# Two of w_out's operands split into halves beside the convolutions, the attention norm's weight folded into w_out, and the steps of the output projection's first pair moved

## The chip, the cores and the metric

The kernel runs on one core of a Trainium2 chip. The metric is the device time of one execution in microseconds. Five engines work side by side, each in the order of its own queue: TensorE (PE, with its weight loads as PEld), VectorE (DVE), ScalarE (ACT), GpSimd (POOL) and SyncE (SP), which here issues the transfers (DMA). Results of TensorE lie in PSUM banks until another engine reads them.

## The reference

One encoder layer on 2048 tokens of width 1024, in float32. The change touches the part from the two norms to the output projection:

```python
att = banded_attention(q_a, k_a, v_a, sink)            # 8 heads of 64
att = rms_norm(att, g_attn_out)                        # (2048, 512)
h_m = rms_norm(h_fwd + h_bwd, g_mlstm_out)             # 4 heads of 128
h_m = sigmoid(o_m) * h_m                               # (2048, 512)
mix = concatenate([att, h_m], axis=-1) @ w_out         # (1024, 1024)
x = x + gate1 * mix
...
```

Ahead of it stand the modulation, the first norm, one input projection, a convolution of width 3 along the tokens for the mLSTM's q and k, the mLSTM in both directions and the banded attention; behind it a SwiGLU layer and the last norm.

## The kernel before

**Arithmetic.** A float32 product is made of three TensorE matmuls of halves (`mm3`, L56 to L58): hi by hi, lo by hi, hi by lo. An operand is split into halves by a ScalarE copy that rounds (hi) and a VectorE subtraction (lo = value − hi).

**Stages**, in the order of TensorE: modulation, first norm and the projections in natural layout (to about 180 us); the convolutions of q and k (about 181 to 243); the mLSTM, head by head (to about 570); the attention (to about 790); the output projection (about 815 to 990); the SwiGLU layer (to the end). Gaps of one stage are filled with matmuls of the next, by a queue `fill` of which `pull(n)` takes n steps. From the convolutions on, VectorE, ScalarE, POOL and SP execute in the order in which the code is written (`manual_schedule`); so where a step stands among the pulls sets its place in each queue.

**The convolutions** run in blocks of 512 tokens: 24 matmuls (L498) into one of two PSUM banks (tag "g"), then ScalarE takes the middle tap out of the bank (L525), ScalarE mends the edges (L526 to L529), and VectorE adds the two outer taps (L512, L513), after which the bank is free for the block after next. A loop of 252 pulls drives this window, and at pull i it also advances two lists of side steps that name their own due pulls by `yield`: `gates()` and `w_out_ops()`.

**w_out's operands.** The output projection is computed with 7 products in place of 8 on 2x2 blocks (a Strassen scheme), for each pair of 128-token blocks: 8 pairs. Its 7 weight operands (u = 0 to 6) are blocks of gate1·w_out and differences of them. `w_out_ops()` makes them in 8 chunks n of 128 rows by 2x256 columns: two loads `bx`, `by`, of w_out's rows of the attention half and of the mLSTM half, a multiplication of each by the gate on POOL (L944, L946), four subtractions on POOL (L957) into `ta` and `tb`, and stores to `wo_d` in DRAM. Chunk n's steps are due from pull 16 + 26n (+10 from n = 4). The two last differences, u = 4 and u = 6, lie in `tb`. The stores of the four differences wait in `out_` until the next chunk (L949), just ahead of the loads for the chunk after that (L922).

**The output projection** (`out_proj`). For product u, `start_wo(u)` loads the operand from `wo_d` as values, and `finish_wo(u)` splits it (L1046 on ScalarE, L1047 on VectorE); u = 5 and u = 6 are split inside the first pair (L1516, L1519). A product is 12 matmuls; b1, b2 and b5 are the three banks in which the seven accumulate, and after each product VectorE adds the bank onto the residual rows `xr` (L1224):

```python
for u, (ps, first, i, m) in enumerate(((b1, True, 0, M0), (b2, True, 0, M0), (b1, False, 0, M1), (b5, True, 1, M1),
                                       (b1, False, 1, M1), (b5, False, 0, M1), (b1, False, 1, M0))):
```

The token operands belong to a `Pair`: `load_a`, `load_m` and `load_gate` load the attention, mLSTM and output gate rows of 256 tokens, `square` and `columns` make the attention's sums of squares (ScalarE L1075, POOL L1076/L1077, TensorE L1125), `scale` multiplies the attention rows by 1/rms and the norm's weight (L1092), `gate` applies the output gate (L1095), `sums`, `s1`, `s4` form block sums on POOL, and `hi`/`lo` split one of the seven operands (L1114 on ScalarE, L1118 on VectorE). While pair p is multiplied, the loop of 28 pulls (i = 0 to 27) prepares pair p+1 (`nxt`) and the sums of squares of p+2 (`nx2`); for p = 0 some of pair 0's own operands are still split in it (`cur.both()`).

Of the kernel before, what the change touches and what calls it, by code (L numbers as in the profile page):

```python
# [36 lines left out]
def hybrid_layer_kernel(  # L37
# [35 lines left out]
    wo_d = dp.tile([7, 4, P, 512], F32, name="wo_d")  # L73
    a_d = dp.tile([7, DFF // P // 2, P, 2, 512], F32, name="a_d")
# [857 lines left out]
    def w_out_ops():  # L932
# [5 lines left out]
        out_ = ()  # L938
        for n, (c_, k) in enumerate(at_):
            at = 16 + 26 * n + 10 * (n > 3)  # L940
            cs = slice(c_ * 256, (c_ + 1) * 256)
            yield at + 3
            bx, by = ready.popleft()
            pool.tensor_tensor(bx, bx, gb[c_], MUL)  # L944
            yield at + 6
            pool.tensor_tensor(by, by, gb[c_], MUL)  # L946
            yield at + 8
            for o in out_:
                sp.dma_start(*o)  # L949
            yield at + 11  # L950
# [3 lines left out]
            tb = s2.tile([P, 2, 256], F32, tag="hst", name="ts")  # L954
            for t, f, g in ((ta[:, 1], bx[:, 1], bx[:, 0]), (tb[:, 0], by[:, 1], bx[:, 1]),
                            (ta[:, 0], by[:, 1], ta[:, 1]), (tb[:, 1], by[:, 0], ta[:, 0])):
                pool.tensor_tensor(t, f, g, SUB)  # L957
# [3 lines left out]
            out_ = [(wo_d[2:4, k, :, cs].rearrange("u p c -> p u c"), ta), (wo_d[4, k][:, cs], tb[:, 0]), (wo_d[6, k][:, cs], tb[:, 1])]  # L961
# [74 lines left out]
    wo = []  # L1036

    def start_wo(u):
        hl = [[big(4 * u + 2 * z + i, "wo") for i in range(2)] for z in range(2)]
        wo.append(hl)  # L1040
        for i in range(2):
            sp.dma_start(hl[1][i].bitcast(F32), wo_d[u, 2 * i:2 * i + 2].rearrange("k p t -> p k t"))
# [8 lines left out]
    class Pair:  # L1051
# [33 lines left out]
        def scale(self):  # L1085
# [5 lines left out]
            for k in range(4):  # L1091
                dve.scalar_tensor_tensor(self.a[:, :, k], self.a[:, :, k], cols[:, O_GA + k:O_GA + k + 1], rb, MUL, MUL)  # L1092
# [143 lines left out]
    nx2.load_m()  # L1236
    nx2.load_gate()
    xr = [load_xr(nxt.tt)]
# [8 lines left out]
    for u in (2, 3):  # L1247
        start_wo(u)
    pull(10)
# [10 lines left out]
    nx2.diagonal(rsqrt(mx, ps[:, :2], 2, 512, "ar"), diag())  # L1260
    finish_wo(2)
    finish_fill(lasts[2])
    for u in (4, 5):
        start_wo(u)
    xr.append(load_xr(nxt.tt + 1))
    nx3.load_a()
    finish_wo(3)
# [3 lines left out]
    finish_wo(4)  # L1271
# [206 lines left out]
    HI, LO = (5, 12, 17, 19, 21, 23, 25), (5, 13, 18, 20, 22, 24, 26)  # L1478
    FIRST = (1, 2, 5, 8, 16, 20, 24)
    rows = None  # L1480
    for p in range(NPR):
# [15 lines left out]
        for i in range(28):  # L1497
# [15 lines left out]
            if p == 0:  # L1513
                if i in (6, 14):
# [449 lines left out]
```

## Time and profile before

| what | value |
|---|---|
| median of 3 runs | 2263.45 us (2263.4, 2265.4, 2263.45) |
| profiled execution | 2268.64 us, span 2266.8 us, mean granted TensorE clock 0.995 |
| TensorE busy | 2223.8 us, 98% |
| VectorE, ScalarE, POOL busy | 1611.1, 1060.3, 1040.6 us (71%, 47%, 46%) |
| DMA | 391.28 MB, 173 GB/s on average |

The span runs from the first to the last record of the profiled execution; some 1.8 us of its time lie around it. In the trace a row is: start, duration (of the whole group where xN stands), engine, line, operation, out<-in, shape, and in brackets the idle time of that engine just before, with what ended it. A window's row has, for each engine, the busy time in the window and the number of instructions, and at its end the granted clock, DMA's busy share and GB/s.

### The profile page before, as it was taken

What the parts mean: (1) busy time and instruction counts of PE and PEld (TensorE: products, weight loads), DVE (VectorE), ACT (ScalarE), POOL (GpSimd) and SP (SyncE); (2) the same over time, 40 slices, a digit from 0 to 9 for tenths busy, and PEclk for the clock granted to TensorE, in tenths of its full rate; (3) what the DMA queues carried; (4) which work ended last, traced back from release to release, by engine and by line L of the source; (5) the groups of instructions that cost most, each with busy time, mean ns of one, the idle gap of its engine ahead of it and who ended that gap; (6) DMA issues with size and microseconds to landing.
All of it is one profiled execution on the core that took longest, in us unless ns stands there. A gap on an engine that the chain in (4) does not pass through costs nothing.

```text
span 2266.8 us, 32424 instructions
## 1 busy us (share of the span) xinstructions
PE 2223.8 (98%) x10822; PEld 1858.7 (82%) x10822; DVE 1611.1 (71%) x2944; ACT 1060.3 (47%) x2206; POOL 1040.6 (46%) x914
## 2 busy tenths in 40 slices
PE   6999999999999999999999999999999999999998
PEld 4997888888888878888888888888888888878887
DVE  6787577656688877886767786766666665785694
ACT  5433565654677746354444444433333333233452
POOL 1006635334344333436666674457566654692020
PEclk9999999999999999999999999999999999999999
DMA  8476755586666576764343454433333374542462
GB/s 329 161 244 209 246 166 168 182 240 180 205 186 183 174 243 207 268 235 150 108 149 112 158 181 164 157 98 111 98 112 98 112 260 142 176 142 94 144 217 93
DMA packets 352811, 391.28 MB, mean 173 GB/s; under 512 B 21260, under 2 KB 251004, under 8 KB 352644
## 3 DMA queue, kind: packets, MB, share of 16 engines
q1 hardware_dynamic: 352420, 389.18, 52.6%
q8 instruction: 85, 1.39, 0.2%
q14 instruction: 82, 0.67, 0.1%
q10 hardware_dynamic: 224, 0.04, 0.0%
HBM read 269.95 MB, written 119.19 MB: 172 GB/s over the span
## 4 chain that ended last, share of the span: by engine, by line
PE 88%; DVE 4%; ACT 3%; DMA 2%; issue 1%; POOL 1%; SPq 0%; ACTq 0%; POOLq 0%; DVEq 0%
PE gps L498 14%; PE fp L56 12%; PE fp L57 12%; PE fp L58 12%; PE fo L56 6%; PE fo L58 6%; PE fo L57 6%; PE ops L56 2%; PE ops L58 2%; PE ops L57 2%; PE kvp L622 1%; PE num L709 1%; PE num L711 1%; PE atp L805 1%; ACT ap L788 1%
## 5 line engine op out<-in xcount | busy, mean ns | idle before, releaser
L498 PE MATMUL gps<-hT,whi 128*128 128x512 f32 x1088 | 396.5, 419 | 0.3 <-DVE cacc L513 0.3
L56 PE MATMUL fo<-w,ah 128*128 128x512 f32 x616 | 239.9, 389 | 1.0 <-DVE rb L1876 1.0
L58 PE MATMUL fo<-w,al 128*128 128x512 f32 x616 | 239.9, 389 | 0.1
L57 PE MATMUL fo<-w,ah 128*128 128x512 f32 x616 | 239.7, 389 | 0.0
L498 PE MATMUL gps<-hT,wlo 128*128 128x512 f32 x544 | 226.7, 417 | 0.0
L498 PEld LDWEIGHTS gps<-hT,whi 128*128 128x128 f32 x1088 | 200.2, 190 | 24.7 <-DVE cacc L513 0.7
L56 PE MATMUL fp<-T,S 128*128 128x512 f32 x528 | 206.7, 391 | 0.3 <-ACT s L1610 0.3
L57 PE MATMUL fp<-T,S 128*128 128x512 f32 x528 | 205.6, 389 | 0.0
L58 PE MATMUL fp<-T,S 128*128 128x512 f32 x528 | 205.4, 389 | 0.0
L1718 DVE TENSOR_TENSOR al<-al,ah 128x1024 fp32r<-128x1024 f32 x77 | 117.4, 1530 | 108.0 <-ACT ah L1717 108.0
L1717 ACT ACTIVATE ah<-al 128x1024 fp32r<-128x1024 f32 x77 | 81.6, 1060 | 182.8 <-DMA al<-a_d 180.3
L1453 DVE TENSOR_TENSOR S<-sf,S 128x512 fp32r<-128x512 f32 x86 | 129.8, 1547 | 34.4 <-ACT S L1452 34.2
L1453 DVE TENSOR_TENSOR A<-graw,A 128x512 fp32r<-128x512 f32 x86 | 130.8, 1541 | 13.2 <-ACT A L1452 12.8
L58 PE MATMUL fp<-B,A 128*128 128x512 f32 x352 | 136.9, 389 | 0.0
L56 PE MATMUL fp<-B,A 128*128 128x512 f32 x352 | 136.9, 389 | 0.0
L57 PE MATMUL fp<-B,A 128*128 128x512 f32 x352 | 136.9, 389 | 0.0
L56 PEld LDWEIGHTS fo<-w,ah 128*128 128x128 f32 x616 | 115.6, 188 | 25.4 <-DVE rb L1876 1.8
L58 PEld LDWEIGHTS fo<-w,al 128*128 128x128 f32 x616 | 115.6, 188 | 24.7 <-DVE al L1718 0.5
L57 PEld LDWEIGHTS fo<-w,ah 128*128 128x128 f32 x616 | 115.6, 188 | 24.2
L1620 DVE SCALAR_TENSOR_TENSOR g<-t,g 128x512 f32<-128x512 f32 x44 | 41.8, 950 | 131.3 <-ACT t L1619 131.3
L798 POOL TENSOR_SCALAR ap<-ap,adn 128x384 f32<-128x384 f32 (+1 forms) x128 | 73.5, 594 | 125.7 <-PE atp L805 58.6
L1457 POOL TENSOR_TENSOR sf<-A,A22r 128x512 f32<-128x512 f32 x42 | 58.1, 1383 | 145.5 <-DMA A22r<-in_w_ffn_in_dram 118.5
(427 smaller groups left out, 6142.2 us busy)
## 6 DMA issues: line engine op xcount, KB each, us to landing
al<-a_d SPq DMA_DIRECT2D x77, 512.0 KB, 3.8
wmod<-in_w_mod_dram SPq DMA_DIRECT2D x48, 512.0 KB, 7.6
graw<-in_w_ffn_in_dram SPq DMA_DIRECT2D x43, 512.0 KB, 3.9
a_d<-ka SPq DMA_DIRECT2D x66, 256.0 KB, 4.7
bc<-bc_d SPq DMA_DIRECT2D x64, 256.0 KB, 3.7
hop_d<-n SPq DMA_DIRECT2D x56, 256.0 KB, 4.0
a_d<-u SPq DMA_DIRECT2D x55, 256.0 KB, 4.6
mqk<-qk_d SPq DMA_DIRECT2D x44, 256.0 KB, 3.8
```

Of the source, the lines that this page charges most:

```text
L56: pe.matmul(o, lh, rh, start=first, stop=False, skip_group_check=skip)
L57: pe.matmul(o, lh, rl, start=False, stop=False, skip_group_check=skip)
L58: pe.matmul(o, ll, rh, start=False, stop=last, skip_group_check=skip)
L498: pe.matmul(ps, w[i == 2][:, k, :], hT[n](i == 1, k), start=(k == 0 and i == 0), stop=(k == KT - 1 and i == 2))
L622: pe.matmul(kvp[:, :129], kn, vw, start=True, stop=True)
L709: pe.matmul(num[:, d, :129], sc[:, d, :], va_c, start=True, stop=st is None)
L798: pool.tensor_scalar(self.p[g][:, :self.NK], self.p[g][:, :self.NK], dn[:, g:g + 1], 0.0, MUL, ADD)
L1453: dve.tensor_tensor(t[:, 1, :], f, t[:, 0, :].bitcast(F32), SUB)
L1457: add.tensor_tensor(f1, a21, a22, ADD)
L1620: dve.scalar_tensor_tensor(g0, t0, 1.0, g0, ADD, MUL)
L1717: act.activation(ah, al.bitcast(F32), AF.Copy)
L1718: dve.tensor_tensor(al, al.bitcast(F32), ah.bitcast(F32), SUB)
```

## The change

1. In `w_out_ops()`, `tb` is split in place: `last_split` copies its two parts to `woh` on ScalarE and subtracts on VectorE, at pull at+5 of the next chunk; the stores of u = 4 and u = 6 go as halves, to `wo_d` (hi) and to a new DRAM tensor `wol_d` (lo). They are four stores where two were.
2. `bx` is multiplied by the attention norm's weight on ScalarE (at+9), between POOL's multiplication and POOL's subtractions. `Pair.scale` loses that factor: four VectorE operations become one, with the 1/rms row broadcast over the four 128-blocks.
3. `start_wo` loads both halves for u = 4 and u = 6; no split of them is left in or ahead of the first pair.
4. Loads ahead of the output projection are issued in another order (u = 2 and 3 before xr and the mLSTM rows; 5 before 4), and the splits of u = 2 and 3 stand one place later.
5. In the first pair, `cur.both()` moves from steps 3, 12, 13 to 0, 2, 13; wo5's subtraction is halved between steps 8 and 11; the squares for pair 2 move from step 15 to 9 (into a buffer of pool `w1`, which therefore lives on to step 22); `gate` and `sums` move by one step, and the `hi`/`lo` steps by one to three.

```diff
     wo_d = dp.tile([7, 4, P, 512], F32, name="wo_d")
+    wol_d = dp.tile([2, 4, P, 512], F32, name="wol_d")
...
         out_ = ()
+
+        cs = None
+
+        def last_split(k, cs, tb):
+            r = []
+            for z, tag in enumerate(("sc", "qs")):
+                hi, lo = s2.tile([P, 256], F32R, tag=tag, name="woh"), tb[:, z]
+                act.activation(hi, lo.bitcast(F32), AF.Copy)
+                dve.tensor_tensor(lo, lo.bitcast(F32), hi.bitcast(F32), SUB)
+                r += [(wo_d[4 + 2 * z, k][:, cs], hi.bitcast(F32)), (wol_d[z, k][:, cs], lo.bitcast(F32))]
+            return r
+
         for n, (c_, k) in enumerate(at_):
             at = 16 + 26 * n + 10 * (n > 3)
...
+            cs_, cs = cs, slice(c_ * 256, (c_ + 1) * 256)
             bx, by = ready.popleft()
             pool.tensor_tensor(bx, bx, gb[c_], MUL)
+            if n:
+                yield at + 5
+                out_ += last_split(at_[n - 1][1], cs_, tb)
             yield at + 6
             pool.tensor_tensor(by, by, gb[c_], MUL)
             yield at + 8
             for o in out_:
                 sp.dma_start(*o)
+            yield at + 9
+            act.activation(bx, bx, AF.Copy, scale=cols[:, O_GA + k:O_GA + k + 1])
             yield at + 11
             if 0 < n < len(at_) - 1:
                 ready.append(w_out_load(*at_[n + 1]))
             ta = s2.tile([P, 2, 256], F32, tag="bc", name="ts", bufs=3)
-            tb = s2.tile([P, 2, 256], F32, tag="hst", name="ts")
-            for t, f, g in ((ta[:, 1], bx[:, 1], bx[:, 0]), (tb[:, 0], by[:, 1], bx[:, 1]),
-                            (ta[:, 0], by[:, 1], ta[:, 1]), (tb[:, 1], by[:, 0], ta[:, 0])):
+            tb = s2.tile([P, 2, 256], F32R, tag="hst", name="ts")
+            tf = tb.bitcast(F32)
+            for t, f, g in ((ta[:, 1], bx[:, 1], bx[:, 0]), (tf[:, 0], by[:, 1], bx[:, 1]),
+                            (ta[:, 0], by[:, 1], ta[:, 1]), (tf[:, 1], by[:, 0], ta[:, 0])):
                 pool.tensor_tensor(t, f, g, SUB)
             yield at + 19
             for u, t in ((0, bx[:, 0]), (1, by[:, 0]), (5, by[:, 1])):
                 sp.dma_start(wo_d[u, k][:, cs], t)
-            out_ = [(wo_d[2:4, k, :, cs].rearrange("u p c -> p u c"), ta), (wo_d[4, k][:, cs], tb[:, 0]), (wo_d[6, k][:, cs], tb[:, 1])]
+            out_ = [(wo_d[2:4, k, :, cs].rearrange("u p c -> p u c"), ta)]
+        yield at + 27
+        out_ += last_split(k, cs, tb)
         yield at + 34
         for o in out_:
             sp.dma_start(*o)
...
+    wo = {}
 
     def start_wo(u):
         hl = [[big(4 * u + 2 * z + i, "wo") for i in range(2)] for z in range(2)]
-        wo.append(hl)
+        wo[u] = hl
         for i in range(2):
-            sp.dma_start(hl[1][i].bitcast(F32), wo_d[u, 2 * i:2 * i + 2].rearrange("k p t -> p k t"))
+            for t, d in ((hl[0], wo_d[u]), (hl[1], wol_d[u // 2 - 2])) if u in (4, 6) else ((hl[1], wo_d[u]),):
+                sp.dma_start(t[i].bitcast(F32), d[2 * i:2 * i + 2].rearrange("k p t -> p k t"))
 
     def finish_wo(u):
         for hi, lo in zip(*wo[u]):
...
-            for k in range(4):
-                dve.scalar_tensor_tensor(self.a[:, :, k], self.a[:, :, k], cols[:, O_GA + k:O_GA + k + 1], rb, MUL, MUL)
+            dve.tensor_tensor(self.a, self.a, rb.unsqueeze(2).to_broadcast([P, 2, 4, P]), MUL)
 
...
     nx2.load_a()
-    nx2.load_m()
-    nx2.load_gate()
-    xr = [load_xr(nxt.tt)]
     ps = bank("a", "aps")
     for i in range(2):
         pe.matmul(ps[:, i:i + 1], nxt.t[:, 2 + i], ones[:, 0:1], start=True, stop=True)
...
         nx2.square(i, sq[:, i])
     for u in (2, 3):
         start_wo(u)
+    xr = [load_xr(nxt.tt)]
+    nx2.load_m()
     pull(10)
     nxt.scale()
     nxt.sums(nxt.t.rearrange("p k t -> p (k t)"))
...
     nx2.diagonal(rsqrt(mx, ps[:, :2], 2, 512, "ar"), diag())
+    finish_fill(lasts[2])
+    start_wo(5)
+    nx2.load_gate()
+    nx3.load_a()
+    xr.append(load_xr(nxt.tt + 1))
+    start_wo(4)
     finish_wo(2)
-    finish_fill(lasts[2])
-    for u in (4, 5):
-        start_wo(u)
-    xr.append(load_xr(nxt.tt + 1))
-    nx3.load_a()
-    finish_wo(3)
     pull(26)
     for _ in range(2):
         nxt.both()
-    finish_wo(4)
+    finish_wo(3)
     while fill:
         pull()
     start_wo(6)
...
     xds = ExitStack()
     HI, LO = (5, 12, 17, 19, 21, 23, 25), (5, 13, 18, 20, 22, 24, 26)
+    HI0, LO0 = (5, 13, 18, 20, 22, 24, 26), (5, 15, 18, 20, 22, 24, 26)
     FIRST = (1, 2, 5, 8, 16, 20, 24)
...
             if p == 0:
-                if i in (6, 14):
-                    for hi, lo in zip(*wo[5 + i // 14]):
+                if i == 6:
+                    for hi, lo in zip(*wo[5]):
                         act.activation(hi, lo.bitcast(F32), AF.Copy)
-                if i in (8, 16):
-                    for hi, lo in zip(*wo[4 + i // 8]):
-                        dve.tensor_tensor(lo, lo.bitcast(F32), hi.bitcast(F32), SUB)
-                if i in (3, 12, 13):
+                if i in (8, 11):
+                    hi, lo = (t[i // 11] for t in wo[5])
+                    dve.tensor_tensor(lo, lo.bitcast(F32), hi.bitcast(F32), SUB)
+                if i in (0, 2, 13):
                     cur.both()
-                if i == 14:
+                if i == 22:
                     w0s.close()
                     xd = xds.enter_context(tc.tile_pool(name="xd", bufs=2, side="left", reuse_waits="tile"))
             if nx2:
-                if i == (1 if p else 15):
-                    sq = [xd.tile([P, 512], F32, tag="n2", name="msq", bufs=9).rearrange("p (k t) -> p k t", k=4) for _ in range(2)]
+                if i == (1 if p else 9):
+                    sq = [(xd.tile([P, 512], F32, tag="n2", name="msq", bufs=9) if p else
+                           w1.tile([P, 512], F32, tag="sq", name="msq")).rearrange("p (k t) -> p k t", k=4) for _ in range(2)]
                     for j in range(2):
                         nx2.square(j, sq[j])
                 if i == at:
...
                 prev.square(1)
             if nxt and i == (1 if p else 4):
...
-            if nxt and i in HI:
+            if nxt and i in (HI if p else HI0):
                 nxt.hi()
-            if nxt and i in LO:
+            if nxt and i in (LO if p else LO0):
                 nxt.lo()
             if nx2 and i == at + 1:
                 parts = [(ps[:, :2], 2, 512)] + ([(prev.ssq, 2, D)] if prev else [])
                 r = rsqrt(mx, parts, 2 * len(parts), None, f"ar{len(parts)}")
                 nx2.diagonal(r, diag())
             if nxt:
-                if i == 11:
+                if i == (11 if p else 12):
                     nxt.gate()
-                if i == 12:
+                if i == (12 if p else 13):
                     nxt.sums(ms2())
```

The first place is ScalarE's queue in the middle of the convolutions. Before, the eviction of a block (`cacc<-gps`) follows the tanh of the block before it (`ctanh`):

```order
L122 ACTIVATE ctanh<-cacc 128x512 [waits DVE_49,Activation_49]
L525 ACTIVATE cacc<-gps,cvb,cvw 128x512 [waits DMAHW5_49,PE_49]
L526 ACTIVATE edge<-gps 128x2
L528 ACTIVATE cacc<-edge,cacc,cvw 128x1 [waits DVE_49,Activation_49]
L529 ACTIVATE cacc<-edge,cacc,cvw 128x1
L122 ACTIVATE ctanh<-cacc 128x512 [waits DVE_49,Activation_49]
```

After, at a place of the same kind, with line numbers one higher, the two copies of a chunk's last differences (`woh<-ts`) and the scale of the next chunk (`bx<-bx,cols`) stand between:

```order
L123 ACTIVATE ctanh<-cacc 128x512 [waits DVE_49,Activation_49]
L947 ACTIVATE woh<-ts 128x256 [waits DMAHW2_49,Pool_49]
L947 ACTIVATE woh<-ts 128x256 [waits DMAHW4_49,Pool_49]
L967 ACTIVATE bx<-bx,cols 128x512 [waits DMAHW0_49,Pool_49]
L526 ACTIVATE cacc<-gps,cvb,cvw 128x512 [waits DMAHW3_49,PE_49]
L527 ACTIVATE edge<-gps 128x2
L529 ACTIVATE cacc<-edge,cacc,cvw 128x1 [waits DVE_49,Activation_49]
L530 ACTIVATE cacc<-edge,cacc,cvw 128x1
```

Three instructions that wait for POOL have moved ahead of an eviction that waits for TensorE.

The second place is SP's queue in the same window: the stores of a chunk's differences (`ts`), the loads of a later chunk (`bx`, `by`), and the stores of the chunk in work. Before:

```order
L949 DMA wo_d<-ts 128x2x256 [waits DMAHW2_49,Pool_49]
L949 DMA wo_d<-ts 128x256 [waits DMAHW3_49]
L949 DMA wo_d<-ts 128x256 [waits DMAHW4_49,Pool_49]
L922 DMA bx<-in_w_out_dram 128x2x256 [waits DMAHW5_49]
L922 DMA by<-in_w_out_dram 128x2x256 [waits DMAHW6_49]
L960 DMA wo_d<-bx 128x256 [waits DMAHW7_49,Pool_49]
L960 DMA wo_d<-by 128x256 [waits DMAHW0_49,Pool_49]
```

After:

```order
L965 DMA wo_d<-ts 128x2x256 [waits DMAHW2_49,Pool_49]
L965 DMA wo_d<-woh 128x256 [waits DMAHW3_49,Activation_49]
L965 DMA wol_d<-ts 128x256 [waits DMAHW4_49,DVE_49]
L965 DMA wo_d<-woh 128x256 [waits DMAHW5_49,Activation_49]
L965 DMA wol_d<-ts 128x256 [waits DMAHW6_49,DVE_49]
L923 DMA bx<-in_w_out_dram 128x2x256 [waits DMAHW7_49]
L923 DMA by<-in_w_out_dram 128x2x256 [waits DMAHW0_49,Pool_49]
L979 DMA wo_d<-bx 128x256 [waits DMAHW1_49,Activation_49]
L979 DMA wo_d<-by 128x256 [waits DMAHW2_49,Pool_49]
```

Ahead of the loads stand two more stores, and the stores of halves wait for ScalarE and VectorE where they waited for POOL.

The third place is VectorE's queue in the first pair of the output projection, from the scaling of the next pair to the add of product 3 (`xr<-xr,ops` is the add of a product, `wo<-wo` half an operand's split, `mA`/`mS` the lo half of a token operand, `mm<-og,mm` the output gate). Before, from the subtraction behind the scaling on:

```order
L1118 TENSOR_TENSOR mA_10415<-ma,mA_10415 128x512 [waits Activation_49]
L1224 TENSOR_TENSOR xr<-xr,ops 128x512 [waits PE_49]
L1519 TENSOR_TENSOR wo<-wo 128x1024 [waits DMAHW4_49,Activation_49]
L1519 TENSOR_TENSOR wo<-wo 128x1024 [waits DMAHW5_49,Activation_49]
L1224 TENSOR_TENSOR xr<-xr,ops 128x512 [waits PE_49]
L1095 SCALAR_TENSOR_TENSOR mm<-og,mm 128x1024 [waits DMAHW1_49,DMAHW0_49]
L1118 TENSOR_TENSOR mS_10450<-mm,mS_10450 128x512 [waits Activation_49]
L1118 TENSOR_TENSOR mA_10461<-mm,mA_10461 128x512 [waits Activation_49]
L1118 TENSOR_TENSOR mA_10453<-mm,mA_10453 128x512 [waits DVE_49]
L1224 TENSOR_TENSOR xr<-xr,ops 128x512 [waits DMAHW6_49,PE_49]
L1519 TENSOR_TENSOR wo<-wo 128x1024 [waits DMAHW2_49,Activation_49]
```

After, from the scaling on (L1113 is the one that L1092 was, L1139 is L1118, L1245 is L1224, L1540 is L1519, L1116 is L1095):

```order
L1113 TENSOR_TENSOR ma<-ma,arb 128x1024 [waits DMAHW7_49,PE_49]
L1139 TENSOR_TENSOR mA_10485<-ma,mA_10485 128x512 [waits Activation_49]
L1245 TENSOR_TENSOR xr<-xr,ops 128x512 [waits PE_49]
L1540 TENSOR_TENSOR wo<-wo 128x1024 [waits DMAHW1_49,Activation_49]
L1245 TENSOR_TENSOR xr<-xr,ops 128x512 [waits PE_49]
L1540 TENSOR_TENSOR wo<-wo 128x1024 [waits DMAHW2_49,Activation_49]
L1116 SCALAR_TENSOR_TENSOR mm<-og,mm 128x1024 [waits DMAHW6_49,DMAHW5_49,DMAHW3_49]
L1139 TENSOR_TENSOR mA_10531<-mm,mA_10531 128x512 [waits Activation_49]
L1245 TENSOR_TENSOR xr<-xr,ops 128x512 [waits DMAHW5_49,PE_49]
```

Between the adds of two products there now stands one half of wo5's split, one subtraction that followed the gate is placed behind the add, and wo6's two are gone.

## The prediction on record

> **What bounds the kernel now.** I read the profile's page first: the span, the busy times of the engines, and the chain of work that ended last.
>
> ```profile
> span 2266.8 us, 32424 instructions
> PE 2223.8 (98%) x10822; PEld 1858.7 (82%) x10822; DVE 1611.1 (71%) x2944; ACT 1060.3 (47%) x2206; POOL 1040.6 (46%) x914
> PE 88%; DVE 4%; ACT 3%; DMA 2%; issue 1%; POOL 1%; SPq 0%; ACTq 0%; POOLq 0%; DVEq 0%
> ```
>
> TensorE is busy 98% of the span and carries 88% of the chain. The change neither adds nor removes a matmul, and TensorE's instructions keep their order. So the time can change only where TensorE waits, or where its clock falls behind a wait. The table of what TensorE waits for (engine and line waited for, total us, times, longest) names three places that the edited lines touch:
>
> ```profile
> PE aps L1125 <- POOL msq L1077: 3.2, 2, 2.1
> PE ops L56 <- ACT msq L1075: 1.6, 1, 1.6
> PE gps L498 <- DVE cacc L513: 0.3, 1, 0.3
> ```
>
> The first two lie at the entry of the output projection, where something is to be won; the third is all that TensorE waits inside the convolutions, where the change puts its new work. The matmuls and two windows show the entry:
>
> ```profile
> 828.91 0.39 PE L57 MATMUL ops<-wo,mS 128*128 128x512 f32 x1
> 829.14 0.39 PE L58 MATMUL ops<-wo,mS 128*128 128x512 f32 x1
> 831.14 0.47 PE L56 MATMUL ops<-wo,mS 128*128 128x512 f32 x1 [1.61 <-ACT msq L1075]
> 831.68 0.40 PE L58 MATMUL ops<-wo,mS 128*128 128x512 f32 x1
> 834.16 0.58 PE L1125 MATMUL aps<-ones_r,msq 128*128 128x1 f32 x2 [2.09 <-POOL msq L1077]
> 835.83 0.58 PE L1125 MATMUL aps<-ones_r,msq 128*128 128x1 f32 x2 [1.08 <-POOL msq L1077]
> 836.28 0.77 PE L56 MATMUL ops<-wo,mS 128*128 128x512 f32 x1
> 840.99 0.40 PE L58 MATMUL ops<-wo,mA 128*128 128x512 f32 x1
> 834.00:836.00 2.00, 0.76 (x3) 0.67 (x4) 1.25 (x2) 0.00 (x0) 1.92 (x4) 0.50 0.00 0
> 805.00:825.00 20.00, 20.00 (x91) 16.45 (x90) 18.40 (x31) 12.37 (x16) 4.02 (x4) 1.00 1.04 350
> ```
>
> Matmuls that don't wait start 0.23 us apart (828.91, 829.14). Three pieces are lost: product 5 was due at 829.37 and starts at 831.14 (1.77); the column sums were due at 831.91 and start at 834.16 (2.25); from there to the next product 836.28−834.16 = 2.12 passes, where the last sum alone takes 0.45 (835.83 to 836.28), so 1.7. And the clock is at 0.50 (third number from the end of the window's row): the eleven steps from 836.28 to 840.99 take 4.71 us in place of 11×0.23 = 2.5, so 2.2 more. In all **7.9 us** are lost here.
>
> **The entry of the output projection: what goes.** These are the instructions ahead of the late ones on VectorE, ScalarE and POOL:
>
> ```profile
> 818.10 0.69 DVE L1224 TENSOR_TENSOR xr<-xr,ops 128x512 f32<-128x512 f32 x1 [0.59 <-PE ops L58]
> 826.28 1.21 DVE L1095 SCALAR_TENSOR_TENSOR mm<-og,mm 128x1024 f32<-128x1024 f32 x1
> 828.71 1.69 DVE L1118 TENSOR_TENSOR mA<-mm,mA 128x512 fp32r<-128x512 f32 x2 [0.62 <-ACT mA L1114]
> 830.32 0.67 DVE L1224 TENSOR_TENSOR xr<-xr,ops 128x512 f32<-128x512 f32 x1
> 828.58 1.99 ACT L1516 ACTIVATE wo<-wo 128x1024 fp32r<-128x1024 f32 x2
> 830.48 1.14 ACT L1075 ACTIVATE msq<-ma 128x512 f32<-128x512 f32 x2
> L1519 DVE TENSOR_TENSOR wo<-wo x4: 1209/1210/1742, 823.4 to 832.1; 128x1024 fp32r<-128x1024 f32 x4
> 819.31 1.65 DVE L1092 SCALAR_TENSOR_TENSOR ma<-ma,cols,arb 128x256 f32<-128x256 f32 x4
> ```
>
> Product 5 accumulates in the bank that the add at 830.32 must empty first; that add stands behind the gate (826.28) and two subtractions (828.71). The trace names ACT at 831.14, but it is this add, ending at 830.99, that comes just ahead. The column sums need the squares of 830.48, which ScalarE runs behind wo6's split of 828.58.
>
> After the change both weight operands, u=4 and u=6, arrive as halves, so wo6's two copies on ScalarE and two subtractions on VectorE go; the four scalings (1.65) become one tensor operation of 128x1024. The trace doesn't show that form: L1519 does the same shape in 1.21, and the four of before are the other end; I take 1.21. Squares are issued at step 9 instead of 15. VectorE's new queue, worked through with these durations from the add of product 0 (818.10+0.69 = 818.8, as now): scaling to 820.0, subtraction behind ScalarE's copy to about 822, add of product 1 by 822.9, half of wo5 (1.21) 824.1, add 824.8, second half 826.0, gate 827.2, subtraction 827.9, add of product 3 **828.6**, or 829.1 if POOL slows one. It is needed at 829.37: no wait. The squares, two ScalarE copies earlier and with nothing of wo6 ahead, leave POOL some 5 us before 831.91, so the sums don't wait either, and with no wait before it the clock stays up. I put the gain at **7.7 us**, 0.2 being left for the sums themselves. Ends: 7.9 if all goes, 5 if one wait and half the slow stretch stay.
>
> The cover of this is the loads. DMA was full until 825 (share 1.04, 350 GB/s). The halves bring 4 more loads of 0.5 MB: 2.1 MB / 350 GB/s = 6.0 us, so the last, wo6, lands at about 831, against a first use at 829.37+2.73 = 832.1. One microsecond is left. The loads and splits that change places ahead of the entry, wo4's copies and subtractions that go there, and the one scaling in the later pairs lie beside matmuls that wait for none of them (no line of the waits names them); I cost them at nothing, and a late wo2 or wo3 would show as a wait for a load.
>
> **The convolutions: what comes.** The steps that make w_out's operands run here, beside 24-matmul blocks that alternate between two PSUM banks. ScalarE empties a bank (L525), two VectorE adds end it (L513):
>
> ```profile
> 224.62 0.78 ACT L525 ACTIVATE cacc<-gps,cvb,cvw 128x512 f32<-128x512 f32 x1 [3.38 <-DMA wo_d<-by]
> 226.35 0.75 DVE L513 SCALAR_TENSOR_TENSOR cacc<-gps,cvw,cacc 128x511 f32<-128x511 f32 x1
> 230.06 0.78 ACT L525 ACTIVATE cacc<-gps,cvb,cvw 128x512 f32<-128x512 f32 x1 [3.38 <-PE gps L498]
> 218.68 1.29 POOL L944 TENSOR_TENSOR bx<-bx,gb 128x512 f32<-128x512 f32 x1 [4.20 <-DMA bx<-in_w_out_dram]
> 224.42 1.56 POOL L957 TENSOR_TENSOR ts<-by,ts 128x256 f32<-128x256 f32 x2
> 227.34 1.74 POOL L944 TENSOR_TENSOR bx<-bx,gb 128x512 f32<-128x512 f32 x1
> 233.69 1.73 POOL L944 TENSOR_TENSOR bx<-bx,gb 128x512 f32<-128x512 f32 x1
> 244.98 1.71 SPq L964 DMA_DIRECT2D wo_d<-ts  x3
> 247.29 0.43 SPq L589 DMA_DIRECT2D mqk<-qk_d  x1
> 251.66 0.41 ACT L617 ACTIVATE vw<-mv,wT 128x129 f32<-128x129 f32 x1 [0.20 <-DMA mv<-vaug_d]
> DMA to landing us min/median/max: 2.9/4.1/5.3
> L681 DVE SCALAR_TENSOR_TENSOR sc<-sps,ng 128x256 f32<-128x256 f32 x1 | 0.4, 417 | 0.0
> L142 DVE TENSOR_TENSOR maccl<-macc,macch 128x512 fp32r<-128x512 f32 x1 | 0.8, 800 | 0.8 <-ACT macch L141 0.8
> L122 ACT ACTIVATE ctanh<-cacc 128x512 f32<-128x512 f32 x12 | 7.3, 620 | 0.9 <-DVE cacc L513 0.9
> L614 ACT ACTIVATE kn<-ktp 128x128 f32<-128x128 f32 x16 | 4.3, 269 | 3.2 <-PE ktp L612 3.0
> 215.00:235.00 20.00, 20.00 (x90) 16.57 (x89) 8.91 (x12) 7.78 (x17) 16.16 (x17) 1.00 0.98 314
> ```
>
> From 224.62 to the end of L513 at 227.10 pass 2.48 us, and the bank is wanted when the next block ends, at 230.06. So an eviction may be 2.96 us late for nothing.
>
> Each of the eight chunks gets one ScalarE scale of bx (128x512: 0.62, by L122), which waits for POOL's multiply and for which POOL's subtractions now wait; two ScalarE copies of 128x256 (0.39, on the line between 0.27 for 128 columns, L614, and 0.62 for 512); two VectorE subtractions of 128x256 (0.42 by L681, 0.80 by L142; 0.42 taken, since it has the shape); and five stores in place of three, 256 KB more, ahead of the next chunk's load in SP's queue.
>
> *ScalarE's queue.* The eviction of 224.62 now stands behind the scale of chunk 5, whose multiply ends at 227.34+1.74 = 229.08. With the scale and 0.1 for semaphores it starts at 229.8, 5.2 late: 2.2 us of wait. The next, of 230.06, stands behind chunk 6's scale: 235.42+0.72 = 236.1, 6.1 late, so TensorE is **3.1 us** behind in all. This holds even if nothing on POOL moves: it is the floor.
>
> *The round trip.* But POOL does move. SP issues chunk n+1's load only behind the stores of chunk n−1's halves, so a round now runs from POOL's last subtraction through a copy, copies' end and subtraction (1.2), the stores (2.5; 0.5 each, by 1.71 for the three at 244.98), landing (4.1) to the multiply (1.3). Chunk 1 is late already, its scale standing behind an eviction; I estimate that chunk 4's load goes out some 3 us later for it, five stores (2.5) being issued where three were, and that chunk 4's subtractions end at 229.1 instead of 225.98 (224.42+1.56). Chunk 5's multiply then ends at 232.2 (229.08+3.1), and its last subtraction 4.6 behind, as now (chunk 6's multiply starts at 233.69), at 236.8. Chunk 6's load goes out at 229.1+1.2+2.5 = 232.8; it has landed at 236.9, and its multiply (1.7) ends at about 239. Chunk 7's load goes out at 236.8+3.7 = 240.5; landed 244.6, multiplied 245.9, ended 4.6 behind at 250.5. Now that end is 244.98, where SP sends the last stores. The eviction behind chunk 6's scale lets its bank go at 239+0.72+2.48 = 242.2, wanted at 230.06+5.44 = 235.5: 6.7 us behind. DMA is full here (0.98, 314 GB/s), so each 256 KB more costs 0.8 us; on the loads of chunks 4 and 7 that is 1.6 more, end 252.1. Behind it SP issues the last chunk's stores, then the first mLSTM loads: 2.3 us now (244.98 to 247.29), plus the halves (1.2) and two more stores (1.1): 256.7, **9.4 us** later than 247.29. That load has no slack: ScalarE waits 0.20 for its companion at 251.66. Nothing behind gives it back while TensorE is the bound. I take 9.4, ends 3.1 and 14.2.
>
> A row bears on the price of the halves: wo6's subtraction takes 1.21 by median and 1.74 at most, with POOL at work beside it. The Trainium skill ("GPSIMD Engine Reference", section "Specifications") says that GpSimd shares its SBUF interfaces with VectorE and contends with VectorE instructions of two SBUF inputs. By that the halves beside POOL's subtractions would cost the upper price, as in the first rival; the trace agrees for L1519.
>
> **Sum.** The profiled run took 2268.64 (span 2266.8 plus 1.84 around it), 5.2 above the median of 2263.45; the terms are differences, so they are carried over to the median: 2263.45 + 9.4 − 7.7 = **2265.2**.
>
> **The rivals.**
> 1. *Slower: the round trip is dearer.* The landing takes 5.3 instead of 4.1 on chunks 4 and 7 (2.4), and the halves 0.80 each, which is 0.8 per round over three rounds (2.4): 14.2 − 7.7, so 2270.0. For it: DMA share 0.98, and POOL's wait of 4.20 at 218.68. Against: what waits also spreads its transfers over more time. It decides once chunk 7's last subtraction ends later than 254.9.
> 2. *The clock falls in the new waits.* At 836 it was 0.50 after waits of 1.77, 2.25 and 1.75 within 7 us, and that cost 2.2. One or two falls between 200 and 250, 2.2 each: 2267.4 to 2269.6. Against: the new waits are spread over blocks of 5.4 us. The Trainium skill ("TensorE: Matmul & The Clock Gate", section "Why this matters for your kernels") advises no idle gaps over about 3 us between bursts. It speaks against this change, and by it the waits of the forecast, 2 to 3 us each, would just escape; the trace shows a fall with no single gap that long.
> 3. *Faster: only the floor is paid.* Loads land early enough that POOL's times stay; then 2.2 to 3.1 against 7.7: 2258.0 to 2258.9. For it: POOL waited 4.20 for chunk 4's load, and such a wait can swallow a scale or a half. Against: the scale and the halves are in series with those loads.
> 4. *The entry doesn't do what it says.* wo6 or wo4 lands 2 to 4 us late, the clock falls again, and the gain is 4: 2268.9. For it: one microsecond of margin. Against: by the window 834 to 836 DMA moves nothing there now, so there is room.
>
> **How the numbers follow.** A measurement of this kernel tells about 0.2% from no change, 4.5 us: the bounds are 2258.9 and 2268.0. Forecast 0.30 (2262 to 2268; 0.285 of it same, 0.015 slower); rival 1 0.28 (0.224 slower, 0.056 same); rival 2 0.10 (half slower, half same); rival 3 0.25 (0.16 faster, 0.09 same); rival 4 0.07 (half and half). That gives faster 0.16, same 0.51, slower 0.33. The range takes in rival 3 down to 2257.5 and rival 1 up to 2271; some 0.08 lie beyond each end.
>
> **What would show it.** At the entry: no wait of TensorE for ACT or POOL behind product 4, the clock at 1.00 throughout, and under 0.5 us lost. In the convolutions: TensorE's wait for L513's successor growing from 0.3 to 7 us or more, evictions idle before them with POOL's multiply as releaser, and chunk 7's last subtraction near 252. The prediction is wrong if that subtraction ends before 247 (rival 3) or after 255 (rival 1), or if wo's tiles are waited for by DMA.

## The result, and the profile after

The changed kernel takes 2269.95 us (median of 12 runs, 2266.67 to 2273.54), against 2265.09 us before (12 runs, 2262.64 to 2267.22): a ratio of 1.0021, 95% interval 1.0013 to 1.0029, so **4.8 us slower**. The forecast was 1.7 slower. The two profiled executions differ less (2268.64 before, 2268.12 after): the one of before lost some 2 us more by 186 us, where its clock stood at 0.50 from 182 on, and 1.5 between 2018 and 2024, both outside the two places of the change. So places are compared by how far the same matmul has shifted from one trace to the other.

First what TensorE waits for, the lines of after that belong to edited code (engine and line waited for, total us, times, longest):

```profile
PE gps L499 <- DVE cacc L514: 6.3, 3, 3.0
...
PE ops L56 <- ACT mA L1135: 1.4, 1, 1.4
...
PE ktp L613 <- ACT kn L615: 0.7, 1, 0.7
...
PE arb L1110 <- DVE dg L1105: 0.4, 1, 0.4
```

The wait of 3.2 for POOL's sums is gone, and the wait inside the convolutions has grown from 0.3 to 6.3 us. In the order of time (TensorE's rows of after, with the two rows of before that they are set against below):

```profile
199.70 0.63 PE L499 MATMUL gps<-hT,whi 128*128 128x512 f32 x2
207.88 0.70 PE L499 MATMUL gps<-hT,whi 128*128 128x512 f32 x2 [2.19 <-DVE cacc L514]
234.53 0.73 PE L499 MATMUL gps<-hT,whi 128*128 128x512 f32 x2 [2.98 <-DVE cacc L514]
241.37 0.73 PE L499 MATMUL gps<-hT,whi 128*128 128x512 f32 x2 [1.10 <-DVE cacc L514]
251.64 0.33 PE L613 MATMUL ktp<-ident,mqk 128*128 128x128 f32 x1 [0.66 <-ACT kn L615]
844.06 0.68 PE L1110 MATMUL arb<-dg,ones_r 128*128 128x128 f32 x4 [0.41 <-DVE dg L1105]
850.27 0.47 PE L56 MATMUL ops<-wo,mS 128*128 128x512 f32 x1 [1.43 <-ACT mA L1135]
```

```profile
202.12 0.74 PE L498 MATMUL gps<-hT,whi 128*128 128x512 f32 x2 [0.27 <-DVE cacc L513]
244.62 0.33 PE L612 MATMUL ktp<-ident,mqk 128*128 128x128 f32 x1
```

The same block starts at 202.12 before and at 199.70 after, 2.42 early; the same transposition at 244.62 and 251.64, 7.02 late. So **9.4 us** are lost between. Four waits make 6.9 of it. Most of the rest is the clock, behind the first of them: a window of 2 us at 0.80 lacks 0.4 us of full clock, one at 0.50 lacks 1.0, one at 0.85 lacks 0.3, in all 1.7 (windows of after; the third number from the end is the granted clock):

```profile
206.00:208.00 2.00, 0.12 (x1) 0.15 (x2) 1.97 (x4) 1.53 (x5) 1.92 (x4) 1.00 0.58 197
208.00:210.00 2.00, 2.00 (x8) 1.59 (x9) 1.85 (x7) 0.43 (x2) 1.16 (x2) 0.80 0.79 218
210.00:212.00 2.00, 2.00 (x6) 1.53 (x5) 1.24 (x2) 0.92 (x2) 1.75 (x2) 0.50 0.81 272
212.00:214.00 2.00, 2.00 (x9) 1.62 (x8) 1.65 (x2) 0.84 (x2) 2.00 (x3) 0.85 0.51 154
836.00:838.00 2.00, 2.00 (x12) 1.73 (x12) 1.85 (x2) 0.63 (x1) 1.92 (x2) 1.00 1.07 356
```

At the entry of the output projection there is no slow clock left (836 to 838 stands at 1.00). What the stage as a whole gained is seen in two rows of each kernel that group its matmuls by form, with the first and the last start; first before, then after:

```profile
L56 PE MATMUL ops<-wo,mA x96: 389/393/628, 815.1 to 989.9; 128*128 128x512 f32 x96
```

```profile
L56 PE MATMUL ops<-wo,mA x96: 389/389/484, 821.8 to 991.2; 128*128 128x512 f32 x96
```

The first product starts 6.7 later, the last matmuls 1.3 later: the stage is 5.4 us shorter.

### The profile page after: what moved, and what is told of

Read it like the earlier page. It is cut to its first block, busy times and chain, and to the rows that moved or that the text cites. A ratio compares the mean times of both kernels' runs of the same rounds, so it can differ in the third digit from the quotient of the medians.

```text
span 2266.3 us, 32498 instructions
## 1 busy us (share of the span) xinstructions
PE 2220.3 (98%) x10822; PEld 1856.5 (82%) x10822; DVE 1610.0 (71%) x2932; ACT 1066.2 (47%) x2226; POOL 1044.2 (46%) x914
## 4 chain that ended last, share of the span: by engine, by line
PE 60%; DVE 1%; DMA 0%; issue 0%; ACT 0%; POOL 0%; DVEq 0%; POOLq 0%; ACTq 0%; SPq 0%
PE fp L56 12%; PE fp L57 12%; PE fp L58 12%; PE fo L58 6%; PE fo L57 6%; PE fo L56 6%; PE ops L56 2%; PE ops L58 2%; PE ops L57 2%; PE trn L1331 0%; PE trn L184 0%; DMA A22r<-in_w_ffn_in_dram 0%; DMA x_d<-xr 0%; DVE xr L1245 0%; DVE B L1434 0%
```

## The experiments

Ratios are to the kernel before, run on the same chip in the same session, with their 95% intervals; 0.001 is 2.3 us. Each kernel was timed in five rounds beside it.

**1. The entry alone.** `w_out_ops()` as before, the rest as changed.

```diff
...
-            for t, d in ((hl[0], wo_d[u]), (hl[1], wol_d[u // 2 - 2])) if u in (4, 6) ...
+            for t, d in ((hl[0], wo_d[u]), (hl[1], wo_d[u])) if u in (4, 6) ...
```

> The changed kernel with the steps beside the convolutions as before: no scale of bx and no halves there; the entry of the output projection as changed, with the lo halves of u = 4 and 6 loaded from the hi operand's place. It leaves out the norm's weight and the true lo halves, but has all loads and instructions of the changed entry. Forecast: what the entry is worth by itself. The three waits and the slow clock of 829 to 841 go (7.5 in the trace), two new waits near 844 and 850 take 1.9 back: -5.6 on before, ratio 0.9975. Rival (the entry gives less when its loads collide with work that is not delayed by the convolutions): -2 or less.

Measured 0.9977 (0.9968 to 0.9986): −5.2 us, as expected. So the work beside the convolutions costs 4.8 + 5.2 = 10.0 us as timed (each of the two is known to about 2 us), and 9.4 by the trace. The two waits that take part of the entry's gain back are there without any delay from the convolutions, so they belong to the changed entry:

```profile
837.61 0.68 PE L1090 MATMUL arb<-dg,ones_r 128*128 128x128 f32 x4 [0.43 <-DVE dg L1085]
843.82 0.47 PE L56 MATMUL ops<-wo,mS 128*128 128x512 f32 x1 [1.40 <-ACT mA L1115]
```

**2. Which part of the work beside the convolutions?** Two kernels take the fold and the halves apart.

```diff
-            yield at + 9
-            act.activation(bx, bx, AF.Copy, scale=cols[:, O_GA + k:O_GA + k + 1])
...
```

> The changed kernel with the norm's weight taken back out of w_out: no ScalarE scale of bx in the convolutions, and four VectorE scalings per pair again; the halves of u = 4 and 6 are still made and stored beside the convolutions. Theory 1 (the scale, waiting for POOL, stands ahead of an eviction in ScalarE's queue): the waits of 2.98 and 1.10 us at 234.5 and 241.4 of the changed kernel go, so about 4.5 us less than it, about level with before (0 to +1). Theory 2 (the halves' round trip through SP and the load carries the cost): the waits stay, within 1 us of the changed kernel, +4 to +5 on before.

> The kernel before with the fold alone: one ScalarE scale of bx per chunk, one VectorE operation in place of four in the scaling of a pair; no halves made early, the entry of the output projection in its old order. Theory 1: TensorE waits behind the evictions that follow the scales of chunks 5 and 6, 2.2 to 3.1 us in all as in the prediction's floor, so +2 to +3 on before. Theory 2: the scale alone falls into the slack of 2.96 us, within 1 us of before.

Without the fold: 1.0030 (1.0019 to 1.0042), no better than the changed kernel; that it is 2 us worse than theory 2 gives is not explained. The fold alone: 1.0003 (0.9994 to 1.0012), not to be told from none, though the interval reaches up to the 2 to 3 us of theory 1. The scale does make waits by itself, as the trace of the fold alone shows (its only ones for an eviction), but small ones:

```profile
229.75 0.74 PE L498 MATMUL gps<-hT,whi 128*128 128x512 f32 x2 [1.51 <-DVE cacc L513]
235.69 0.73 PE L498 MATMUL gps<-hT,whi 128*128 128x512 f32 x2 [0.21 <-DVE cacc L513]
```

In the traces TensorE loses 1.7 us beside the convolutions with the fold alone and 9.6 without the fold, against 9.3 in the changed kernel (table behind experiment 4). So theory 1 falls as the main cause: the **halves** carry it. In the kernel without the fold the eviction waits behind the halves' copy instead of behind a scale (ScalarE's rows there):

```profile
229.39 0.42 ACT L947 ACTIVATE woh<-ts 128x256 fp32r<-128x256 f32 x1 [5.82 <-POOL ts L974]
230.97 0.42 ACT L947 ACTIVATE woh<-ts 128x256 fp32r<-128x256 f32 x1 [1.17 <-POOL ts L974]
231.30 0.77 ACT L526 ACTIVATE cacc<-gps,cvb,cvw 128x512 f32<-128x512 f32 x1
```

ScalarE stands idle for POOL's late differences with an eviction behind it. POOL is late since its loads are: the load of chunk 4 goes out at 219.31 there and POOL multiplies from 223.58, 4.3 behind it; before, the two were 214.24 and 218.68, 4.4 apart.

**3. The stores ahead of the loads.** Two kernels test the round trip from two sides: the loads moved ahead of the stores in SP's queue (with step 25 of experiment 5), and half of the halves' stores left out.

```diff
             yield at + 8
+            if 0 < n < len(at_) - 1:
+                ready.append(w_out_load(*at_[n + 1]))
             for o in out_:
                 sp.dma_start(*o)
...
             yield at + 11
-            if 0 < n < len(at_) - 1:
-                ready.append(w_out_load(*at_[n + 1]))
```

> The changed kernel with step 25 as in the run before, and with the loads of the next chunk's bx and by issued on SP ahead of the stores of a chunk's differences and halves. Round-trip theory (the loads stand behind stores that wait for ScalarE's and VectorE's halves): the loads go out 5 to 7 us earlier, as in the kernel before, and the cost beside the convolutions falls from about 10 us to 3 (1.7 behind the scales, about 1 behind chunk 1's halves), so -3 on before. Rival (the engines' queues carry it: halves and scale stand ahead of the evictions wherever the loads are): +2 or more on before.

> The changed kernel with one store per operand and chunk instead of two: the halves are made beside the convolutions as changed, but only one of them is stored, and is loaded for both. It leaves out the true hi halves; ScalarE's and VectorE's work is that of the changed kernel, SP issues three stores per chunk of differences as before, 1 MB less is stored. If the number of stores ahead of the loads is the cost, the loads go out 1 us earlier per round and 2 to 3 us of about 10 go: +2 to +3 on before. If the wait for the halves is the cost, within 1 us of the changed kernel, +4 to +5.

Loads first: 1.0002 (0.9993 to 1.0011). One store per operand: 1.0007 (0.9998 to 1.0016). Against the 1.0021 of the changed kernel, timed in another session, both are some 3 to 4 us faster, and the first does not reach the −3 that was expected of it; the second comes nearest to what the number of stores was expected to give.

The traces bear this out for one store, not for the loads first. The loads do go out earlier: that of chunk 6, at 227.29 before, is 7.3 us late in the changed kernel, 3.7 with one store and 3.8 with the loads first (each counted from the matmul that starts at 200.18 before). But TensorE, which loses 9.3 us beside the convolutions in the changed kernel and 7.5 with one store, loses 9.3 with the loads first as well (table behind experiment 4): its waits have moved, and the clock falls twice. So the round trip carries a part of the cost, and without it the halves' other places in the queues come up. With the loads first no wait is left between 215 and 245, but two remain at the edges of the window:

```profile
209.30 0.69 PE L499 MATMUL gps<-hT,whi 128*128 128x512 f32 x2 [2.28 <-DVE cacc L514]
250.71 0.33 PE L613 MATMUL ktp<-ident,mqk 128*128 128x128 f32 x1 [3.00 <-ACT kn L615]
```

The clock falls behind both (0.57 and 0.58 in 210 to 212 and 212 to 214, 0.56 and 0.59 in 251 to 253 and 253 to 255). The first stands behind VectorE's halves, the second behind ScalarE, which waits for a weight load whose issue on SP stands behind the stores (VectorE, ScalarE and SP in that run; the row of SP is the load's issue):

```profile
205.45 2.26 DVE L948 TENSOR_TENSOR ts<-ts,woh 128x256 fp32r<-128x256 f32 x2 [1.29 <-ACT woh L947]
207.63 0.74 DVE L513 SCALAR_TENSOR_TENSOR cacc<-gps,cvw,cacc 128x511 f32<-128x511 f32 x1
246.88 1.06 ACT L252 ACTIVATE whi<-wraw 128x1024 fp32r<-128x1024 f32 x1 [5.04 <-DMA wraw<-in_w_in_dram]
240.93 0.46 SPq L248 DMA_DIRECT2D wraw<-in_w_in_dram  x1
```

**4. Other places for the same work.** Loads first, with four further edits: no fold; the scale ahead of POOL's multiplication; that with the halves 14 steps later; and the halves set by hand behind an eviction.

```diff
+    def halves():
+        for y in (58, 82, 106, 154, 178, 202, 226):
+            yield y
+            put_halves()
...
```

> As the run with the loads first, but with the norm's weight taken back out of w_out (no scale of bx, four VectorE scalings per pair). Round-trip theory: only the halves stay, 1 to 2 us beside the convolutions, -4 to -5 on before. Rival: no better than the run with the loads first.

> As the run with the loads first, with the scale of bx placed ahead of POOL's multiplication, so that ScalarE waits for the load alone and not for POOL's turn. Round-trip theory: the waits of 1.5 to 3 us behind the scales of chunks 5 and 6 go, -4 to -5 on before. Rival (ScalarE now waits for loads that land late, with the eviction behind it): no better than the run with the loads first.

> As the run before it, with the halves of a chunk's last differences made 14 steps later (step 19 of the next chunk instead of 5) and stored at its step 25, so that POOL has long made them when ScalarE comes to them. If an eviction still waits behind the halves, this takes it away: -5.5 on before, the gain of the entry alone plus the 1.4 of step 25, less about 1. Rival: no better than the run before it, since nothing waits there any more.

> The run with the loads first, with the halves placed by hand 10 steps behind an eviction instead of 5 steps into the next chunk, stored at once, and the last chunk's halves 24 steps into the mLSTM. If place in the queues is what costs (VectorE's halves ahead of L514 at 209, ScalarE's ahead of the evictions, SP's stores ahead of the weight load that ScalarE waits for at 247), the two waits of 2.3 and 3.0 us and the slow clock behind them go: -4 to -5 on before. If POOL and VectorE simply get in each other's way, about half stays: -2.

Measured 1.0022 (1.0013 to 1.0030), 1.0013 (1.0004 to 1.0022), 1.0011 (1.0002 to 1.0020) and 1.0022 (1.0013 to 1.0030): none saved what the round trip theory gave, the rival of the first three (no better than the loads first) holds, and the last misses both of its cases. Each shifts a wait to another place. In the last one the stores follow the halves at once, and so stand ahead of the next loads again; the load that went out at 220.62 in the kernel before goes out at 224.69, though that run is 2.7 us early at 200, and the wait is back behind a scale:

```profile
224.69 0.56 SPq L923 DMA_DIRECT2D bx<-in_w_out_dram  x1
231.82 0.72 ACT L979 ACTIVATE bx<-bx,cols 128x512 f32<-128x512 f32 x1 [5.60 <-POOL bx L970]
234.96 1.22 PE L499 MATMUL gps<-hT,whi 128*128 128x512 f32 x2 [3.15 <-DVE cacc L514]
```

That the kernel without the fold and with the loads first is slower than the one with it (1.0022 against 1.0002) is not explained; its trace only shows that it loses 2.4 us more beside the convolutions (table below), in waits at 203.8, 211.3, 246.5 and 254.0.

The table has, for each kernel so far and that of experiment 5, what TensorE loses against before beside the convolutions: how much the matmul at 260.02 before, behind the last slow clock there, has shifted against the one at 200.18. (The kernel before has a wait of 0.27 itself at 202.12, and the end lies 15 us later, so the changed kernel has 9.3 here and not 9.4.)

| kernel | lost beside the convolutions (us) | ratio timed |
|---|---|---|
| changed | 9.3 | 1.0021 |
| changed, step 25 (experiment 5) | 8.9 | 1.0018 |
| entry alone | 0.3 | 0.9977 |
| fold alone | 1.7 | 1.0003 |
| without the fold | 9.6 | 1.0030 |
| one store | 7.5 | 1.0007 |
| loads first | 9.3 | 1.0002 |
| loads first, no fold | 11.7 | 1.0022 |
| loads first, scale ahead | 10.7 | 1.0013 |
| the same, halves later | 8.9 | 1.0011 |
| loads first, halves by hand | 13.3 | 1.0022 |

A second execution of the same code (step 25) gives nearly the same loss. The 3 to 4 us that the loads first save as timed are not in this place, and where they are is not found. One execution can differ by a microsecond or two from the median, so the table tells what happens beside the convolutions, and the ratios what the whole takes.

**5. One step of the second pair.**

```diff
-    HI0, LO0 = (5, 13, 18, 20, 22, 24, 26), (5, 15, 18, 20, 22, 24, 26)
+    HI0, LO0 = (5, 13, 18, 20, 22, 24, 25), (5, 15, 18, 20, 22, 24, 26)
```

> The changed kernel with one number changed: the hi copy of the last operand of the second pair at step 25 instead of 26, so ahead of the squares of the finished rows (L1310) in ScalarE's queue. If that place causes the wait of 1.43 us at 850.27, it goes: 1.4 less than the changed kernel, +3.4 on before. If the wait belongs to the scaling (L1113 at 848.32), it stays, within 0.5 of the changed kernel.

Measured 1.0018 (1.0009 to 1.0027), 0.7 us under the changed kernel, which the intervals don't separate. The trace does: no wait is left at that matmul (it starts at 851.90 there, without a bracket).

```profile
851.90 0.48 PE L56 MATMUL ops<-wo,mS 128*128 128x512 f32 x1
853.17 0.38 PE L1146 MATMUL aps<-ones_r,msq 128*128 128x1 f32 x2 [0.21 <-POOL msq L1099]
```

So the wait of 1.43 came from the hi copy that went from step 25 to 26, behind the squares of the finished rows; its worth in time is not settled.

**6. The moved steps without the halves.** The kernel before, with the order of the first pair changed much as in the change and nothing else: wo4 is split where it was, and wo6 still inside the first pair.

```diff
-                if i in (8, 16):
-                    for hi, lo in zip(*wo[4 + i // 8]):
-                        dve.tensor_tensor(lo, lo.bitcast(F32), hi.bitcast(F32), SUB)
-                if i in (3, 12, 13):
+                if i in (8, 11, 17, 19):
+                    hi, lo = (t[i in (11, 19)] for t in wo[5 + i // 17])
+                    dve.tensor_tensor(lo, lo.bitcast(F32), hi.bitcast(F32), SUB)
+                if i in (1, 3, 13):
                     cur.both()
...
```

> The kernel before with only the moved steps of the first pair: squares at step 9, two token operands earlier (steps 1 and 3), gate and sums one step later, wo5's subtraction at 8 and 11, wo6's at 17 and 19, the second pair's hi and lo as changed, with step 25. No halves made early, no fold; wo4 and wo6 are still split where they were, nothing new beside the convolutions. Theory A (order, not work, made the waits at the entry): the waits of 831 and 834 and the slow clock go, -4 to -6 on before, ratio 0.9975 to 0.998, and it beats both kernels. Theory B (the freed work of wo4 and wo6 is needed): a wait of 1 to 2 us stays at product 5 and the clock falls again, -1 to -3.

Measured 0.9981 (0.9972 to 0.9989): −4.3 us, faster than before and than the changed kernel. Theory A holds: order made the waits of 831 and 834. Three waits are new, 0.23 at 839.04, 0.55 at 844.40, and a long one of product 6 for the add of product 4 behind wo6's subtraction; the clock stands behind it undiminished:

```profile
829.74 2.31 DVE L1520 TENSOR_TENSOR wo<-wo 128x1024 fp32r<-128x1024 f32 x1
831.98 1.75 DVE L1118 TENSOR_TENSOR mS<-ma,mS 128x512 fp32r<-128x512 f32 x1
833.65 0.67 DVE L1224 TENSOR_TENSOR xr<-xr,ops 128x512 f32<-128x512 f32 x1
834.46 0.47 PE L56 MATMUL ops<-wo,mA 128*128 128x512 f32 x1 [2.52 <-ACT mS L1114]
833.00:837.00 4.00, 2.54 (x11) 2.13 (x12) 3.97 (x8) 2.31 (x4) 1.85 (x2) 1.00 0.00 0
```

The last kernel moves those two subtractions to steps 15 and 19:

> The moved steps alone, with wo6's two subtractions at 15 and 19 instead of 17 and 19, ahead of the token operands' lo halves, so that the add of product 4 no longer stands behind them (2.52 us of wait at 834.5 in the moved steps' trace). Theory A: that wait falls to 0.5 or less and nothing else moves: 2 us less than the moved steps, -6.5 to -7 on before. Rival: the lo halves moved behind make another wait, within 1 us of the moved steps.

Measured 0.9979 (0.9970 to 0.9988), not to be told from 0.9981: the rival. The wait of 2.52 becomes 0.89, and 1.91 appears at the next pair's row broadcast:

```profile
834.61 0.47 PE L56 MATMUL ops<-wo,mA 128*128 128x512 f32 x1 [0.89 <-DVE xr L1224]
840.89 0.68 PE L1088 MATMUL arb<-dg,ones_r 128*128 128x128 f32 x4 [1.91 <-DVE dg L1083]
```

Of the kernels that compute the whole layer these two are the fastest run; the entry alone, at 0.9977, leaves out the norm's weight and the true lo halves.

## Why the prediction was right or wrong

The measured 2269.95 lies inside the range (2257.5 to 2271.0) around the predicted 2265.2. Of the 4.8 us between the two, 1.6 are the base (2263.45 from three runs then, 2265.09 from twelve now) and 3.1 the net, +4.8 where +1.7 was forecast. By the prediction's own bound of 0.2% the likeliest class, "same", is missed narrowly: 0.21% slower, with an interval (0.13 to 0.29%) that takes in both. The direction of the net was right.

**What bounds the kernel, and where it can change:** right. The two places carry the difference: −5.2 at the entry, +10.0 in the convolutions.

**The entry, 7.7 gained:** right as far as it went. Product 5 and the sums start without a wait and the clock stays at 1.00. In the trace this is 7.8 us: the first product is 6.7 late at 815.1, and behind the old slow stretch the same matmul is 1.1 early, first before, then after:

```profile
841.22 0.39 PE L56 MATMUL ops<-wo,mA 128*128 128x512 f32 x1
```

```profile
840.08 0.39 PE L56 MATMUL ops<-wo,mA 128*128 128x512 f32 x1
```

The step that failed is the list behind it, which looked only at what goes. The moved hi and lo steps of the second pair were put at nothing; they were not walked past the row squares in ScalarE's queue, and 2.3 us come back around 844 and 850, 1.8 of them in the two waits. The wait at 850 is shown to come from step 26 (experiment 5); what makes the one at 844 was not tested. Net 5.5, and 5.4 over the stage.

**The floor, 3.1 behind the scales of chunks 5 and 6:** too high as a floor. The fold alone, whose trace is that case, waits 1.7 and loses as much.

**The round trip, 9.4:** the number was met (9.4 in the trace, 10.0 as timed), and the chain is in the trace: loads behind the stores of the halves, POOL behind the loads, evictions behind POOL. Its times were close. They are set against before as TensorE's are, so 2.4 us are added to each time of after: chunk 6's load goes out at 232.61, so 235.0 (232.8 predicted), chunk 7's at 239.40, so 241.8 (240.5), chunk 7's last subtraction ends at 249.03, so 251.4 (252.1), and the mLSTM load goes out at 254.81, so 257.2 (256.7). The first row below is what SP waits for between 196 and 256:

```profile
SPq L965 <- ACT woh L947: 6.4, 2, 4.6
239.40 0.56 SPq L923 DMA_DIRECT2D bx<-in_w_out_dram  x1
247.47 1.56 POOL L976 TENSOR_TENSOR ts<-by,ts 128x256 f32<-128x256 f32 x2
204.01 2.27 DVE L948 TENSOR_TENSOR ts<-ts,woh 128x256 fp32r<-128x256 f32 x2 [1.29 <-ACT woh L947]
254.81 0.45 SPq L590 DMA_DIRECT2D mqk<-qk_d  x1
```

But the last step, from the chain to the time, failed. The prediction took the lateness of the mLSTM load, which has no slack there, for what TensorE loses. TensorE has lost its 9.4 us at 251.64 already, 3 us ahead of that load's issue, and the trace lists no further wait of it up to 300. It lost them in the convolutions: 6.3 us behind evictions, 0.7 behind ScalarE, 1.7 to the clock. For the evictions the prediction has 6.7, all behind the scales of chunks 5 and 6; the runs show 4.1 there, and 2.2 at 207.88 behind the halves of chunk 1, a place of which the prediction only says that chunk 1 is late. That this path and the load's path both come to 9.4 is luck.

The price of the halves failed too: 0.42 was taken and 0.80 held as the other end. The pair at 204.01, beside POOL, took 1.40 and 0.95, and stands ahead of the two adds of an eviction; that made the wait of 2.19.

**Rival 2, the clock:** it came, once: from 209 to 213, 1.7 us, inside the 9.4. The forecast gave it 0.10 and took it as an addition; it was part of the sum by accident. The advice of the Trainium skill ("TensorE: Matmul & The Clock Gate", section "Why this matters for your kernels"), no idle gaps over about 3 us, would have let a wait of 2.19 pass; the trace has the fall behind it. **Rival 1** names a time, 2270.0, that is the measured one, by another sum: its 14.2 was not reached (9.4 to 10.0), and its sign, chunk 7's last subtraction later than 254.9, did not come. It had the halves dear, as they were, but in the loop to chunk 7. **Rival 3** is refuted in the changed kernel. **Rival 4** did not come as described: wo's operands are waited for by no DMA; the gain fell short of 7.7 for the moved steps instead.

What the prediction did not ask is whether the halves were needed for the entry. Mostly they were not: order alone, with step 25, takes the waits of 831 and 834 away and gains 4.3 us as timed, where the changed entry gained 5.2, and the intervals overlap. By the trace, order alone gains 3.8 over the stage against 5.4 (6.3 with step 25), its new wait of 2.52 behind wo6's subtraction being the main part of what it lacks.

## What to carry to other kernels

Work that is moved to a stage with idle engines still takes a place in four in-order queues there, and a costly place may be on the queue that does no arithmetic: stores that wait for a late product hold up the loads behind them. Before paying for work to be moved away from a waiting engine, try the order of what stands ahead of the late instruction; and walk every moved step past what it now stands behind, also in the iteration after the one that is looked at.

## What the runs showed of the hardware

The clock fell to 0.50 behind single waits of TensorE of 2.19 us (the changed kernel), 2.28 and 3.00 (loads first), and cost about 1.7 us each time; it did not fall behind waits of 2.98 (the changed kernel, at 234.53) and 2.52 (the moved steps). So the length of a wait alone does not tell it, between 2.2 and 3 us. And in the changed kernel a VectorE subtraction of 128x256 took 0.41 to 0.43 us where POOL was idle for most of it, and 0.42 to 1.51 beside POOL's work.
